# Second feed-forward product in three groups of 8, 8 and 6 hidden chunks, all by seven products, the last group ordered by token half

## The chip, the cores and the metric

The kernel runs on one core of a Trainium2 chip. The metric is the time of one execution on the device in microseconds. The three runs shown took 1502.62, 1504.49 and 1505.2 us; their median is 1504.49 us. All traces and rows below are from one profiled execution.

## The reference

One block of a streaming encoder, batch 1, 1024 tokens, width 1024, float32. A gated mixing sub-layer comes first, then the feed-forward sub-layer, whose end the change touches, and a last normalisation:

```python
h2 = rms_norm(x, norm_ffn_g[l]) * (1.0 + sc2) + sh2
a, bgate = jnp.split(jnp.einsum('bsd,df->bsf', h2, w_ffn_in[l]), 2, axis=-1)
x = x + g2 * jnp.einsum('bsf,fd->bsd', jax.nn.silu(a) * bgate, w_ffn_out[l])
...
return rms_norm(x, final_norm_g)
```

The hidden width is 2816, that is 22 chunks of 128. The second einsum (2816 to 1024) is "the second feed-forward product".

## The kernel before

Activations lie transposed: 128 channels on the partitions, tokens along the free axis, in two token halves of 512. Every float32 operand is split into a rounded high part and a low rest, and one product of 128x128 weights with 128x512 activations is three matmuls: weight high with activation high (L283), weight high with activation low (L284), weight low with activation high (L286). ScalarE makes the high part of a weight tile `wh` (L205), VectorE the low part `wl` (L206), from a loaded tile `raw`. The pools `wh` and `wl` have three buffers each, and `next_w` prepares weights two products ahead (`AHEAD = 2`).

Large products are made by **seven products** in the place of eight (Strassen's scheme, in the variant that shares its sums). A 2x2 block product has output rows (two blocks of output channels) and columns (two token halves); the seven are named by the characters of `PRODUCTS = "1265734"`. `product` (L295) makes one of them for two output chunks p = 0 and 1, over a number of hidden chunk pairs, in a PSUM bank: 1, 6, 7 and 4 accumulate in a bank called x, 2 in y, 5 and 3 in z. After each, VectorE adds the bank's content, scaled, to the residual tile `x1[j]` (L1013, called an evacuation here). Products 1 and 2 complete output chunk j = 2d + p in the first token half and 4 completes chunk j + 4 there; 6 and 3 go to chunk j, 5 and 7 to chunk j + 4, in the second half (d, 0 or 1, is the pair of output chunks). The next product that accumulates in a bank must wait for the evacuation before it.

The feed-forward part runs in these steps. (1) The first feed-forward product: eleven pairs of hidden chunks, N_IN = 11, seven products each, 24 matmuls a product (`in_product`). After a pair, `hid_set` (L932) forms the seven activation operands of the second product from its results, splits each into a staging tile (pool `stage`, three buffers; ScalarE L322, VectorE L323) and stores it to DRAM by a DMA that GpSimd (POOL) issues (L930). (2) The residual x1 is loaded again from DRAM: chunks 0 and 1 early, chunks 4, 5, 2, 3, 6 and 7 by six DMAs of POOL (L1006), after `hid_set` of the last pair. (3) The second product for hidden chunks 0 to 17, in three groups of three pairs: `group_load` (L961) brings a group's operands, two tiles `th` and `tl` for each pair and product, from DRAM by POOL's queue (L956), and then come seven products of 18 matmuls for d = 0 and seven for d = 1. The tiles `th`, `tl` come from a pool `t` of 58 buffers, which the operands of step 1 (56 tiles) and all the groups share; group 0's loads follow the first feed-forward product's last pair, product by product. (4) The last four hidden chunks (18 to 21) are multiplied directly (L1055, `piece_out`), in three pieces of the tokens, `PIECES = [(0, 512), (512, 256), (768, 256)]`: 12 matmuls for each of eight output chunks j and each piece.

With a piece's eighth chunk the last normalisation of that piece begins: ScalarE has squared the outputs (L1067), VectorE summed the squares (L1076), a matmul with ones sums over partitions (`ss`, L1104), ScalarE takes the reciprocal root and VectorE refines it in two steps (`rft` L1113, `rf` L1115). Then `piece_scale` (L1078) multiplies each chunk by `rf`: in pieces 0 and 1 all eight chunks on POOL (L1092), in the last piece chunks 0, 3 and 5 on POOL and five on VectorE (L1094). The results leave by DMAs of SyncE (L1097). Piece i is normalised while piece i + 1 is being multiplied.

The order on each engine is laid down when the kernel is built: a scheduler places instructions by priority and readiness, and each engine then takes its own list strictly in order. POOL's DMAs share eight semaphores in turn, so a DMA waits in the list until the eighth before it has landed.

## Time and profile before

| what | us |
|---|---|
| median of the runs (1502.62 to 1505.2) | 1504.49 |
| the profiled execution, its own time | 1502.96 |
| its span in the trace | 1501.2 |
| what lies around the span | 1.76 |
| busy: PE, VectorE, ScalarE, POOL | 1469.3, 1141.0, 623.1, 538.2 |

Times in rows are microseconds from the span's start. PE is TensorE, DVE VectorE, ACT ScalarE, POOL GpSimd and SP SyncE. A timeline row gives start, duration, engine, line, operation, output<-input and shape; in brackets stands how long the engine was idle before it and what ended that. Matmuls are pipelined, so that a row of 0.39 us and the next one's start overlap: the pitch, from start to start, is what a matmul costs.

### The profile page before, as it was taken

How to read it: one execution, taken by the hardware profiler on the slowest of the kernel's cores; microseconds unless marked ns; L12 is line 12 of the kernel's file. 1: busy time of each engine (PE TensorE's matmuls, PEld its weight loads, DVE VectorE, ACT ScalarE, POOL GpSimd, SP SyncE). 2: the span in 40 equal slices, each digit the busy share in tenths (PEclk: the TensorE clock that was granted, in tenths of full speed). 3: DMA queues.
4: the chain of work that ended last, by engine and by line, in shares of the span. 5: the costliest groups of instructions: out<-in, count | busy, mean ns of one | idle time of the engine just before them, and what ended most of it. 6: DMA issues, size and time to landing. Idle time of an engine off the chain costs nothing.

```text
span 1501.2 us, 17711 instructions
## 1 busy us (share of the span) xinstructions
PE 1469.3 (98%) x6455; PEld 1202.0 (80%) x6455; DVE 1141.0 (76%) x1569; ACT 623.1 (42%) x896; POOL 538.2 (36%) x467
## 2 busy tenths in 40 slices
PE   6999999999999999999999989999999999999997
PEld 2788888888888788887788868888888888888887
DVE  7994999887887984777767789776666665667755
ACT  4653433443343353244345454444444443222235
POOL 0037777777767773410121001111000016444005
PEclk9999999999999999999999989999999999999999
DMA  9522223232222268555765337544444449998403
GB/s 352 207 64 74 94 71 112 70 108 75 98 71 85 99 261 299 167 175 175 231 207 183 126 98 236 200 169 153 152 149 150 153 148 351 364 324 256 141 28 112
DMA packets 82697, 247.24 MB, mean 165 GB/s; under 512 B 9521, under 2 KB 11697, under 8 KB 82610
## 3 DMA queue, kind: packets, MB, share of 16 engines
q1 hardware_dynamic: 41776, 137.91, 27.4%
q0 software_dynamic: 36944, 95.44, 19.2%
q10 hardware_dynamic: 3890, 12.78, 2.2%
q8 instruction: 50, 0.82, 0.2%
q14 instruction: 37, 0.30, 0.1%
HBM read 183.69 MB, written 62.39 MB: 164 GB/s over the span
## 4 chain that ended last, share of the span: by engine, by line
PE 93%; DVE 4%; issue 1%; ACT 1%; DMA 1%; POOL 0%; POOLq 0%; ACTq 0%; DVEq 0%
PE x L286 11%; PE x L284 11%; PE x L283 10%; PE z L283 7%; PE z L284 7%; PE z L286 7%; PE y L284 6%; PE y L283 6%; PE y L286 6%; PE ya L284 2%; PE mix L286 2%; PE mix L284 2%; PE ya L283 2%; PE ya L286 2%; PE mix L283 2%; PE yb L283 2%
## 5 line engine op out<-in xcount | busy, mean ns | idle before, releaser
L205 ACT CAST wh<-raw 128x1024 fp32r<-128x1024 f32 (+2 forms) x257 | 259.4, 1010 | 482.8 <-PE z L284 122.0
L206 POOL TENSOR_TENSOR wl<-raw,wh 128x1024 fp32r<-128x1024 f32 x92 | 227.2, 2471 | 131.1 <-ACT wh L205 130.9
L206 DVE TENSOR_TENSOR wl<-raw,wh 128x1024 fp32r<-128x1024 f32 (+2 forms) x165 | 188.4, 1142 | 52.7 <-ACT wh L205 50.0
L671 DVE SCALAR_TENSOR_TENSOR c<-diff,vec,c 128x512 f32<-128x512 f32 x248 | 178.6, 751 | 3.3
L930 POOL DMA_DIRECT2D hid<-stage x71 | 37.9, 534 | 358.7 <-DVE stage L323 353.0
L283 PE MATMUL x<-th,wh 128*128 128x512 f32 x240 | 93.4, 389 | 0.0
L284 PE MATMUL x<-tl,wh 128*128 128x512 f32 x240 | 93.4, 389 | 0.0
L286 PE MATMUL x<-th,wl 128*128 128x512 f32 x240 | 93.4, 389 | 0.0
L671 DVE SCALAR_TENSOR_TENSOR c<-u,wsum,c 128x512 f32<-128x512 f32 x112 | 84.1, 751 | 1.8
L264 DVE CUSTOM_DVE_ANT_0 raw<-raw,cs,vec 128x1024 f32<-128x1024 f32 x24 | 35.5, 1486 | 50.6 <-DMA raw<-in_ada 50.6
L283 PE MATMUL z<-th,wh 128*128 128x512 f32 x168 | 65.4, 389 | 0.0
L284 PE MATMUL z<-tl,wh 128*128 128x512 f32 x168 | 65.4, 389 | 0.0
L286 PE MATMUL z<-th,wl 128*128 128x512 f32 x168 | 65.4, 389 | 0.0
L228 POOL TENSOR_TENSOR raw<-raw 128x1024 f32<-128x1024 f32 x12 | 29.8, 2482 | 95.0 <-DVE wl L206 94.2
L322 ACT CAST stage<-g 128x512 fp32r<-128x512 f32 x62 | 38.3, 621 | 52.0 <-DMA hid<-stage 25.1
L323 DVE TENSOR_TENSOR stage<-g,stage 128x512 fp32r<-128x512 f32 x62 | 42.5, 688 | 20.5 <-ACT stage L322 20.4
L956 POOL DMA_DIRECT2D th<-hid x71 | 38.1, 537 | 52.0 <-PE x L286 28.3
L283 PE MATMUL yb<-zsh,wh 128*128 128x512 f32 x128 | 50.0, 391 | 2.8 <-DVE gb L793 2.8
L283 PE MATMUL x<-t2h,wh 128*128 128x512 f32 x120 | 47.7, 400 | 5.1 <-ACT wh L205 2.8
L286 PEld LDWEIGHTS x<-th,wl 128*128 128x128 f32 x240 | 45.1, 188 | 9.4
L283 PEld LDWEIGHTS x<-th,wh 128*128 128x128 f32 x240 | 45.1, 188 | 9.3
L284 PEld LDWEIGHTS x<-tl,wh 128*128 128x128 f32 x240 | 45.1, 188 | 9.3
(1012 smaller groups left out, 4263.8 us busy)
## 6 DMA issues: line engine op xcount, KB each, us to landing
hid<-stage POOLq DMA_DIRECT2D x71, 512.0 KB, 4.0
raw<-in_w_fi SPq DMA_DIRECT2D x50, 512.0 KB, 4.3
raw<-in_w_duals SPq DMA_DIRECT2D x48, 512.0 KB, 3.5
th<-hid POOLq DMA_DIRECT2D x71, 256.0 KB, 5.9
tl<-hid POOLq DMA_DIRECT2D x71, 256.0 KB, 6.0
ada<-in_ada SPq DMA_DIRECT2D x24, 512.0 KB, 5.8
raw<-in_ada SPq DMA_DIRECT2D x24, 512.0 KB, 4.5
raw<-in_w_fo SPq DMA_DIRECT2D x24, 384.0 KB, 6.2
```

Of the source, the lines that this page charges most:

```text
L205: nc.scalar.copy(wh, raw)
L206: lo = lo_engine.tensor_tensor(wl, raw, f32(wh), ALU.subtract)
L228: eng.tensor_tensor(a["s1"], a["21"], a["22"], ALU.add)
L264: nc.vector.tensor_tensor_reduce(out=raw, in0=raw, in1=cs, scale=1.0, scalar=col(V_ADA, b), op0=ALU.mult, op1=ALU.add, accum_out=modc(b),)
L283: nc.tensor.matmul(ps, wh, xh, start=first, stop=False, skip_group_check=again)
L284: nc.tensor.matmul(ps, wh, xl, start=False, stop=False, skip_group_check=again)
L286: mm3.ins = nc.tensor.matmul(ps, wl, xh, start=False, stop=last, skip_group_check=again).ins
L322: nc.scalar.copy(hi, src)
L323: nc.vector.tensor_tensor(lo, src, f32(hi), ALU.subtract)
L671: tap.ins = nc.vector.scalar_tensor_tensor(out=out, in0=src[:, s : s + H], scalar=wt, in1=acc, op0=ALU.mult, op1=ALU.add).ins
L930: nc.gpsimd.dma_start(hid_dram[key], s)
L956: nc.gpsimd.dma_start(t, hid_dram[key][:, s])
```

## The change

The four direct chunks go. All 22 hidden chunks are now taken by seven products, in groups of four, four and three pairs: a product of groups 0 and 1 has 24 matmuls in the place of 18, its weight tiles are 128x1024 in the place of 128x768, and a group brings 56 operand tiles in the place of 42. `hid_set` makes seven stores for each of the eleven pairs (before, four for the last two). The last group has an order of its own: for d = 0 and then d = 1 the products 1, 2, 6, 7 and 4, which complete the first token half in all eight chunks, then product 5 for both d, then product 3, which is made in two pieces of 256 tokens (72 matmuls of 128x256). Its weights come by `last_units`, which loads some blocks again. Piece 0's sums are complete after product 4 and its scaling stands behind the second product 5; pieces 1 and 2 now hold four output chunks' products each.

```diff
-GROUP, GROUPS = 3, 3
-REST = 2 * GROUP * GROUPS
+GROUPS = [range(4), range(4, 8), range(8, 11)]
+LAST_ORDER = [(d, m) for d in range(2) for m in "12674"] + [(d, m) for m in "53" for d in range(2)]
...
+    def last_units(mats, n):
+
+        a = {}
+
+        def unit(m):
+            get = lambda i: load(mats[i], n)
+            add = lambda o, b: nc.vector.tensor_tensor(o, o, b, ALU.add)
+            if m == "6":
+                s, a21, t = get(3), get(2), get(0)
+                add(s, a21)
+                add(a21, t)
+                add(t, s)
+                a["7"] = a21
+            elif m == "5":
+                t, a21 = get(3), get(2)
+                add(t, a21)
+                a["5"] = t
+            elif m == "3":
+                t, a11 = get(1), get(0)
+                add(t, a11)
+                add(t, a["5"])
+            else:
+                t = a[m] if m in a else get("12_4".index(m))
+            return split_w(t, n)
+
+        return {m: (lambda m=m: unit(m)) for m in PRODUCTS}
...
     def hid_set(d):
 
         (b11, b12), (b21, b22) = ((ha[2 * d + p, "4"], ha[2 * d + p, "6"]) for p in range(2))
-        if 2 * d >= REST:
-            for p, half in enumerate(((b11, b12), (b21, b22))):
-                for h in range(2):
-                    store((2 * d + p, h), half[h])
-            return
...
     def group_load(g, m):
-        to[g, m] = [t_load((g * GROUP + i, m)) for i in range(GROUP)]
+        to[g, m] = [t_load((d, m)) for d in GROUPS[g]]
...
-    hid = {}
-    n = 2 * GROUP * P
...
-    for g in range(GROUPS):
-        for d in range(2):
-            banks = {}
-            for m in PRODUCTS:
-                product(banks, m, to[g, m], out_evac(d))
-                if d == 0 and m == "1":
-                    if g < GROUPS - 1:
-                        for q in PRODUCTS:
-                            group_load(g + 1, q)
-                    else:
-                        for h in range(2):
-                            for f in range(REST, FC):
-                                hid[f, h] = t_load((f, h))
-
-
-    ws = {}
-    for f in range(REST, FC, 2):
-        for oh in range(2):
-            raw = load(w_last[(f - REST) // 2, oh])
-            for d in range(2):
...
+    w_fo = [w_fo0, w_fo1, w_fo2]
+    fo_order = [[(d, m) for d in range(2) for m in PRODUCTS]] * 2 + [LAST_ORDER]
+    for g, order in enumerate(fo_order):
+        n = 2 * len(GROUPS[g]) * P
+        units = [(last_units if g == 2 else dual_units)([w_fo[g][d, m] for m in range(4)], n) for d in range(2)]
+        plan += [units[d][m] for d, m in order]
+
+    def out_product(g, d, m):
+        product(fo_banks[g, d], m, to[g, m], out_evac(d))
+
+    fo_banks = {(g, d): {} for g in range(3) for d in range(2)}
+    for g in range(2):
+        for d, m in fo_order[g]:
+            out_product(g, d, m)
+            if (d, m) == (0, "1"):
+                for q in PRODUCTS if g == 0 else "1267453":
+                    group_load(g + 1, q)
...
-    def piece_out(i, j):
-        at, n = PIECES[i]
-        h, off = at // H, at % H
-        o = ps_tile("y")[:, :n]
-        for f in range(REST, FC):
-            xs = tuple(t[:, off : off + n] for t in hid[f, h])
-            c0 = (j % 4) * P
-            mm3([o], slice(c0, c0 + P), ws[f, j // 4], [xs], f == REST, f == FC - 1)
...
-        evac = nc.vector.scalar_tensor_tensor(out=dst, in0=o, scalar=modc(40 + j), in1=dst, op0=ALU.mult, op1=ALU.add)
...
             load_rsqrt(act.ins)
...
+        for k in range(i, i + (n + PIECES[i][1] - 1) // PIECES[i][1]):
...
-    for i in range(len(PIECES)):
-        acc, sqs = sqs[0] if i else None, []
-        lag = LAG if i == LAST else 0
-        for j in range(KC):
-            piece_out(i, j)
-            if j > lag and j - lag < KC - APART * (i == LAST):
-                piece_sum(i, j - lag)
-            if i and j == NORM_AT:
-                norm = piece_norm(i - 1, [acc])
-            if i and j == NORM_AT + 2:
-                with tc.issue_after(piece_out.ins):
-                    rf = piece_rstd(i - 1, *norm)
-                piece_scale(i - 1, rf)
-    piece_scale(LAST, piece_rstd(LAST, *piece_norm(LAST, [sqs[0]] + sqs[KC - APART :])))
...
+    norm = rf = None
+    for d, m in LAST_ORDER[:-2]:
+        out_product(2, d, m)
+        for p in range(2):
+            j = 2 * d + p
+            if m == "2":
+                piece_square(0, j)
+                if j:
+                    piece_sum(sqs[0, 0], sqs[0, j])
+            elif m == "4":
+                piece_square(0, KH + j)
+                piece_sum(sqs[0, 0], sqs[0, KH + j])
+            elif m == "5":
+                piece_square(1, KH + j, H)
+                if j:
+                    piece_sum(sqs[1, KH], sqs[1, KH + j])
+        if (d, m) == (0, "5"):
+            norm = piece_norm(0, [sqs[0, 0]])
+        elif (d, m) == (1, "5"):
+            piece_scale(0, piece_rstd(0, *norm))
+    last = [next_w(), next_w()]
+    for i in (1, 2):
+        at, n = PIECES[i]
+        off = at - H
+        acc = sqs[1, KH][:, off : off + n]
+        for j in range(KH):
+            ps = fo_banks[2, j // 2]["z", j % 2][:, off : off + n]
+            for k, (hi, lo) in enumerate(to[2, "3"]):
+                c0 = (j % 2 * len(to[2, "3"]) + k) * P
+                xs = hi[:, off : off + n], lo[:, off : off + n]
+                mm3([ps], slice(c0, c0 + P), last[j // 2], [xs], False, k == len(to[2, "3"]) - 1, True)
+            dst = x1[j][:, at : at + n]
+            nc.vector.scalar_tensor_tensor(out=dst, in0=ps, scalar=modc(40 + j), in1=dst, op0=ALU.mult, op1=ALU.add)
+            piece_square(i, j)
+            if i < LAST or j < KH - APART:
+                piece_sum(acc, sqs[i, j])
+            if i == LAST and j == NORM_AT:
+                norm = piece_norm(1, [sqs[1, KH][:, : PIECES[1][1]]])
+            if i == LAST and j == NORM_AT + 1:
+                piece_scale(1, piece_rstd(1, *norm))
+    piece_scale(LAST, piece_rstd(LAST, *piece_norm(LAST, [acc] + [sqs[LAST, j] for j in range(KH - APART, KH)])))
```

In the rows below, taken from the lists of the built programs, the numbers behind names tell buffers apart.

**The six loads of x1 on POOL.** Here `hidN_m` is a stored operand of pair N for product m, `th`/`tl` are tiles of group 1, and `x14` to `x17` are x1's chunks 4 to 7 (`x12` chunk 2). Before:

```order
L956 DMA th_9878<-hid3_1_7749 128x512
L956 DMA tl_9879<-hid3_1_7749 128x512
L930 DMA hid21_1_9805<-stage_9802 128x1024
L956 DMA th_9882<-hid4_1_8038 128x512
L956 DMA tl_9883<-hid4_1_8038 128x512
L956 DMA th_9886<-hid5_1_8327 128x512
L1006 DMA x14_9822<-x1_dram4_5820 128x1024
L1006 DMA x15_9823<-x1_dram5_5821 128x1024
```

And of the change:

```order
L978 DMA th_9952<-hid4_1_8038 128x512
L957 DMA hid10_5_9856<-stage_9853 128x1024
L957 DMA hid10_7_9862<-stage_9859 128x1024
L957 DMA hid10_3_9867<-stage_9864 128x1024
L978 DMA tl_9953<-hid4_1_8038 128x512
L957 DMA hid10_4_9873<-stage_9870 128x1024
L978 DMA th_9956<-hid5_1_8327 128x512
L978 DMA tl_9957<-hid5_1_8327 128x512
L1028 DMA x14_9890<-x1_dram4_5820 128x1024
L1028 DMA x15_9891<-x1_dram5_5821 128x1024
```

Ahead of x1's chunk 4 there now stand all seven stores of the last pair, and the tiles `th_9956` and `tl_9957`. These two take the buffers of group 0's first operand tiles (`th_9534`, `tl_9535` below), so they wait until PE has used those for the last time, which is in product 1 of d = 1; `tl_9957` waits for that product's 15th matmul.

**The middle of group 0 on PE.** The banks are x (`x_9938` for d = 0, `x_10265` and `x_10279` for d = 1), y (`y_10297`, d = 1) and z (`z_10017` before, `z_10131` after, d = 0). Before, product 3 of d = 0 follows product 7:

```order
L286 MATMUL x_9867<-th_9701,wl_9989 128x512
L283 MATMUL z_10017<-th_9733,wh_10013 128x512
L284 MATMUL z_10017<-tl_9734,wh_10013 128x512
L286 MATMUL z_10017<-th_9733,wl_10014 128x512
L283 MATMUL z_10017<-th_9737,wh_10013 128x512
```

In the change product 1 of d = 1 and the first 13 matmuls of its product 2 stand between:

```order
L313 MATMUL x_9938<-th_9741,wl_10097 128x512
L310 MATMUL x_10265<-th_9534,wh_10197 128x512
L311 MATMUL x_10265<-tl_9535,wh_10197 128x512
L310 MATMUL x_10279<-th_9534,wh_10197 128x512
L311 MATMUL x_10279<-tl_9535,wh_10197 128x512
L313 MATMUL x_10265<-th_9534,wl_10198 128x512
...
L310 MATMUL y_10297<-th_9594,wh_10227 128x512
L311 MATMUL y_10297<-tl_9595,wh_10227 128x512
L310 MATMUL z_10131<-th_9773,wh_10127 128x512
```

Products 3 and 4 of d = 0 have moved behind these 37 matmuls, while their weights already hold two of the three buffers of `wh` and of `wl`.

**Piece 0's normalisation on VectorE.** `sq` are squares, `ss`, `rq`, `rft` and `rf` the steps of the root. Before, the steps stand among piece 1's evacuations (L1064) of chunks 3 and 4, with 12 evacuations of 256 tokens still to come:

```order
L1064 SCALAR_TENSOR_TENSOR x13_9821<-y_11396,mod_103,x13_9821 128x256
L1076 TENSOR_TENSOR sq_11351<-sq_11351,sq_11392 128x256
L1113 SCALAR_TENSOR_TENSOR rft_11414<-ss_11372,rq_11374 128x512
L1076 TENSOR_TENSOR sq_11351<-sq_11351,sq_11410 128x256
L1115 SCALAR_TENSOR_TENSOR rf_11373<-rft_11414,rf_11373 128x512
L1064 SCALAR_TENSOR_TENSOR x14_9822<-y_11433,mod_103,x14_9822 128x256
```

In the change they stand behind the last evacuation of product 5 of d = 1 (`z_11406`), ahead of the first of product 3's eight:

```order
L1035 SCALAR_TENSOR_TENSOR x17_9893<-z_11406,ng2_9875,x17_9893 128x512
L1083 TENSOR_TENSOR sq_11371<-sq_11371,sq_11417 128x512
L1120 SCALAR_TENSOR_TENSOR rft_11425<-ss_11379,rq_11381 128x512
L1083 TENSOR_TENSOR sq_11371<-sq_11371,sq_11421 128x512
L1122 SCALAR_TENSOR_TENSOR rf_11380<-rft_11425,rf_11380 128x512
L1157 SCALAR_TENSOR_TENSOR x10_9879<-z_11349,mod_103,x10_9879 128x256
```

What follows `rf` has become shorter: eight evacuations of 256 tokens in the place of twelve. POOL's list behind it is the same as before: eight passes of 128x512, eight of 128x256 and three of 128x256 for the last piece.

More of the change, by code (lines that the diff above doesn't have):

```diff
@@ L108, in block_kernel @@
 def block_kernel(ctx: ExitStack, tc: tile.TileContext, x0, xT, c, vecs, ada, w_first, w_plain, w_duals,
-                 w_short, w_conf, w_o, w_fi, w_fo, w_last, outT):
+                 w_short, w_conf, w_o, w_fi, w_fo0, w_fo1, w_fo2, outT):
     nc = tc.nc
@@ L1188 @@
         "w_fi": _duals(w_fi, [[FC + f for f in range(FC)], list(range(FC))], [range(KC // 2), range(KC // 2, KC)]),
-        "w_fo": np.stack([_duals(w_fo, [range(4), range(4, 8)], [range(f, f + 2 * GROUP, 2), range(f + 1, f + 2 * GROUP, 2)])
-                          for f in range(0, REST, 2 * GROUP)]),
-        "w_last": w_fo[REST * P :].reshape(-1, 2, P, 2, H).transpose(0, 3, 2, 1, 4).reshape(-1, 2, P, 1024),
+        **{f"w_fo{g}": _duals(w_fo, [range(4), range(4, 8)], [[2 * d + h for d in ds] for h in range(2)])
+           for g, ds in enumerate(GROUPS)},
     }
```

26 lines of the change are left out of this document (11 added, 15 removed).

## Prediction, written before the change was run

> **What bounds the kernel now.** I read the page's first line and its chain first, then windows and timelines of the two places that the change touches.
>
> ```profile
> span 1501.2 us, 17711 instructions
> PE 1469.3 (98%) x6455; PEld 1202.0 (80%) x6455; DVE 1141.0 (76%) x1569; ACT 623.1 (42%) x896; POOL 538.2 (36%) x467
> PE 93%; DVE 4%; issue 1%; ACT 1%; DMA 1%; POOL 0%; POOLq 0%; ACTq 0%; DVEq 0%
> ```
>
> PE is the bound: busy 98% of the span and 93% of the chain that ends last. So matmuls taken away count in full, unless something else is late in their place. The two places:
>
> ```profile
> 1235.00:1273.45 38.45, 38.45 (x171) 31.84 (x170) 20.58 (x26) 14.97 (x23) 22.66 (x43) 1.00 1.07 331
> 1273.45:1293.85 20.40, 20.40 (x91) 16.90 (x90) 11.68 (x16) 6.24 (x10) 10.24 (x20) 1.00 1.12 385
> 1471.00:1491.00 20.00, 20.00 (x166) 19.84 (x165) 14.36 (x28) 12.77 (x28) 13.80 (x12) 1.00 0.30 114
> 1491.00:1501.20 10.20, 1.93 (x10) 1.29 (x8) 3.40 (x8) 1.77 (x5) 5.20 (x8) 0.80 0.54 190
> ```
>
> Columns: window, length, busy time of PE, PEld, DVE, ACT and POOL, granted clock, DMA share, GB/s. Until 1491 PE is never idle. Around group 0's start (1273.45) all 16 DMA engines are full, at 331 and 385 GB/s. The last 10.2 us have almost no PE work. The chain's own end:
>
> ```profile
> 1469.60 0.87 PE ss L1104 x2
> 1481.98 0.60 PE ss L1104 x2
> 1488.69 5.41 POOL y L1092 x7
> 1494.11 1.17 issue
> 1495.27 0.77 POOLq L1199
> 1496.04 1.37 POOL y L1092 x2
> ```
>
> POOL's scaling is already the last part of the chain: it has next to nothing to spare, although it is busy 36% of the whole.
>
> **Part A: fewer matmuls.**
>
> ```profile
> 1273.45 0.39 PE L283 MATMUL x<-th,wh 128*128 128x512 f32 x1
> 1277.53 0.39 PE L283 MATMUL y<-th,wh 128*128 128x512 f32 x1
> 1482.66 0.28 PE L286 MATMUL y<-th,lwl 128*128 128x256 f32 x1
> 1490.92 0.28 PE L286 MATMUL y<-th,lwl 128*128 128x256 f32 x1
> ```
>
> From the first row to the second lie 18 matmuls: pitch 0.2267 us. From the third to the fourth lie 69: pitch 0.1197 us. Before, from 1273.45 on: 42 products of 18 are 756, and the direct chunks add 96 of 512 and 192 of 256 tokens: 171.4 + 21.8 + 23.0 = 216.1 us. After: 28 products of 24 and 12 of 18 are 888, and product 3 is 72 of 256: 201.3 + 8.6 = 209.9 us. **Part A is −6.2 us.**
>
> **Part B: POOL's passes become the tail's bound.**
>
> ```profile
> 1475.94 10.79 POOL L1092 TENSOR_TENSOR x<-x,rf 128x512 f32<-128x512 f32 x8 [82.49 <-DVE rf L1115]
> 1487.99 6.11 POOL L1092 TENSOR_TENSOR y<-x,rf 128x256 f32<-128x256 f32 x8 [1.26 <-DVE rf L1115]
> 1495.31 2.10 POOL L1092 TENSOR_TENSOR y<-x,rp 128x256 f32<-128x256 f32 x3 [1.20 <-ACT rp L1083]
> 1474.18 0.69 DVE L1113 SCALAR_TENSOR_TENSOR rft<-ss,rq 128x512 f32<-128x512 f32 x1
> 1475.11 0.68 DVE L1115 SCALAR_TENSOR_TENSOR rf<-rft,rf 128x512 f32<-128x512 f32 x1
> ```
>
> POOL's list behind piece 0's `rf` is unchanged: 10.79 + 6.11 + 2.10 = 19.0 us of passes. Before, it begins at 1475.94, 15.1 us ahead of PE's last direct matmul (1490.92 + 0.12 = 1491.04), and its gaps of 1.26 and 1.20 us are its slack. The change puts the start behind the second product 5, with only product 3 (8.6 us of PE) to cover it. Without a stall that product ends at 1273.45 + 201.3 + 0.9 (two `ss` matmuls, as in the chain) = 1475.6. Then `rf` needs the last evacuation (0.75, L1013's length below), a sum of squares (0.69), `rft` (0.69), another sum (0.69) and `rf` (0.68), in VectorE's order as shown above, with 0.2 of hand-over: **3.7 us**. Then 0.15, 19.0 of passes without a gap, and 3.8 from the end of POOL's last pass to the span's end, as before (1495.31 + 2.10 = 1497.41 to 1501.2). End: 1475.6 + 26.65 = 1502.3. Bounded by PE it would be 1475.6 + 8.6 + 0.6 (the second `ss` pair) + 10.2 = 1495.0. So POOL gives back 7.3 us, and **A and B together are +1.1 us**. Unknown are the 3.7 us: 3.4 if every step follows without a gap, 4.6 if ScalarE's root adds 0.9 that the sums don't hide.
>
> [...]
>
> **Part S: a stall in the middle of group 0.** These six loads of x1 fed product 5 of d = 0:
>
> ```profile
> 1274.98 1.07 POOL L930 DMA_DIRECT2D hid<-stage  x2 [0.72 <-DVE stage L323]
> 1284.33 0.56 POOL L1006 DMA_DIRECT2D x<-x_dram  x1
> 1288.28 2.62 POOL L1006 DMA_DIRECT2D x<-x_dram  x5 [3.39 <-issue]
> DMA to landing us min/median/max: 6.0/7.7/8.8
> 1292.50 0.75 DVE L1013 SCALAR_TENSOR_TENSOR x<-z,ng,x 128x512 f32<-128x512 f32 x1 [4.95 <-DMA x<-x_dram]
> 1293.85 0.39 PE L283 MATMUL z<-th,wh 128*128 128x512 f32 x1
> ```
>
> Chunk 4 was issued at 1284.33 and evacuated bank z (p = 0) at 1292.50 to 1293.25, after 4.95 us of VectorE waiting for it. PE wanted the bank at 1293.85: a margin of 0.60 us, with no wait on PE. In the change these loads stand behind seven stores and behind `tl_9957`, which waits for the 15th matmul of product 1 of d = 1. Product 3 of d = 0, which needs bank z, comes only 22 matmuls later.
>
> ```profile
> L206 DVE TENSOR_TENSOR wl<-raw,wh 128x1024 fp32r<-128x1024 f32 x15 | 18.4, 1223 | 13.8 <-ACT wh L205 13.4
> L205 ACT CAST wh<-raw 128x1024 fp32r<-128x1024 f32 x15 | 15.8, 1051 | 23.8 <-PE z L284 13.4 <-PE x L284 5.6 <-PE y L284 4.5
> ```
>
> Step by step: products 1, 2, 6, 5 and 7 of d = 0 are 120 matmuls and end at 1273.45 + 27.2 = 1300.65. Two of three buffers of `wh` and `wl` hold the postponed weights of 3 and 4, so the weights of product 1, d = 1, can be made only then: 1.05 us of cast, then 1.22 of low part, of which PE's first matmuls cover 0.9: 1.05 + 0.3 or so. VectorE makes that low part behind the staging of the last store, which I put at 0.8 us more. Product 2 of d = 1 meets the same want of a buffer: some 1 us again. The place and the count come from the order, the prices from the rows: about **3 us** of PE idle. `tl_9957` is then free at about 1307 (1300.65 + 2.2 + 15 × 0.2267, and its issue), x1's chunk 4 is issued at about 1307.4, and lands 6.0 to 8.8 us later by the row above; that was beside full queues, and 512 KB took 3.5 to 4.0 elsewhere:
>
> ```profile
> hid<-stage POOLq DMA_DIRECT2D x71, 512.0 KB, 4.0
> raw<-in_w_duals SPq DMA_DIRECT2D x48, 512.0 KB, 3.5
> hid<-stage POOLq DMA_DIRECT2D x8, 512.0 KB, 5.5
> ```
>
> With 4 to 8 us and 0.75 of evacuation the bank is free at 1312.2 to 1316.2. PE reaches product 3 at 1300.65 + 3 + 37 × 0.2267 = 1312.0. That adds 0 to 4 us. I take 2, nearest to the 5.5 of stores in this stage, so **S = 5 us** (3 to 7). What could lengthen it: the first of the seven stores. Until it can be issued, 54 tiles of 256 KB, 6 stores and 7 weight tiles of 512 KB, 21 MB, must pass from 1238.2 on. At 385 GB/s that takes 54.5 us. Then the seven are spread as VectorE stages them; in an earlier pair they went out like this:
>
> ```profile
> 1198.22 0.53 POOL L930 DMA_DIRECT2D hid<-stage  x1 [23.25 <-DVE stage L323]
> 1202.49 1.74 POOL L930 DMA_DIRECT2D hid<-stage  x3 [3.74 <-DVE stage L323]
> 1207.24 0.53 POOL L930 DMA_DIRECT2D hid<-stage  x1 [3.02 <-DVE stage L323]
> 1211.36 0.53 POOL L930 DMA_DIRECT2D hid<-stage  x1 [2.23 <-DVE stage L323]
> ```
>
> 13.1 us from first to last issue. If the first goes out at 1285 to 1288, the last does by 1301 and `tl_9957` decides. If it comes later, the loads come later one for one.
>
> [...]
>
> **What costs nothing.** Six more stores (0.53 us of POOL each) lie in the first product, where POOL waits 23 us for staging. Weight tiles of 1024 cost cast 1051 ns against 5.4 us of PE a product. The last group's VectorE work has little room:
>
> ```profile
> L206 DVE TENSOR_TENSOR wl<-raw,wh 128x768 fp32r<-128x768 f32 x42 | 39.9, 951 | 0.8 <-ACT wh L205 0.8
> ```
>
> 14 low parts and 12 weight sums of this width by 0.95, 24 evacuations by 0.75 and 10 sums of squares by 0.69 are 49.6 us, some 45 from start to start (a row overlaps the next by about 0.08), beside 12 × 18 × 0.2267 = 49 us of PE. It fits if each evacuation comes within the 2 us that the other chunk's nine matmuls give it. If that cover is too thin, products there start 0 to 2 us late; I add nothing, since the range has room for it.
>
> **Sum.** Span 1501.2 + 1.1 + 5 = 1507.3; own time 1502.96 + 6.1 = 1509.1. The median of the runs shown is 1.5 above the profiled one, so 1510.6; rounded down, for VectorE's gaps, to **1510.0**.
>
> **Rivals**, in own time of a profiled execution.
>
> R1, not slower: POOL keeps up. If the 19 passes took up to 11.7 us in the place of 19.0, PE would set the tail, 1495.0 in the span without a stall; with a stall of 3 to 5 us that is 1499.8 to 1501.8. Against it stands POOL's row, 1.35 us a pass of 512; the price of 7.3 us falls away from 0.83 us a pass on. For it: only that POOL has 1.2 us idle twice. Chance 0.08, half of it faster than before by over 0.2%, that being about what a measurement of this kernel can tell from no change.
>
> R2, the stall is small: x1 lands in 4 us and VectorE makes the low parts at once, S = 0 to 2, 1504 to 1506. Against it: two buffers are held. 0.10.
>
> R3, the loads come later: stores first at 1291 to 1296, by 363 GB/s or VectorE's staging beside the evacuations; S = 8 to 14, 1512 to 1518. For it: 4.95 us of waiting already, and the mean of the windows above, 350 GB/s. 0.22.
>
> R4, the change does only what the count says: no stall, POOL not late, 1496.8. POOL's rows and the order speak against it. 0.05.
>
> Forecast, S = 3 to 7, 1507 to 1511: 0.55.
>
> **How the numbers follow.** 0.2% of 1504.5 is 3.0 us: 1501.5 and 1507.5 in medians, 1500.0 and 1506.0 in own time. Faster: R4 and about half of R1, 0.08. Same: the rest of R1, R2, 0.15. Slower: the forecast and R3, 0.77. The range 1503.5 to 1517 leaves out R4, R1 and the top third of R3, 0.20 in all.
>
> **What would show it.** A: 888 matmuls of 512 at 0.2267 from group 0's start, 72 of 256 behind them. B: POOL's 19 passes without a gap of over 0.3 us at the end, on the chain of waits. S: PE idle some 1 us ahead of products 1 and 2 of d = 1 in group 0, released by ScalarE's `wh`, and 1 to 4 us ahead of product 3, released by VectorE's evacuation that waits for x1. It is wrong if POOL idles in the tail, if PE shows no such gaps, or if new gaps lie in groups 1 or 2.

## The result, and the profile after

The changed kernel takes 1516.52 us in the median of four runs (1513.58 to 1518.51), against 1504.76 before: the ratio is 1.0081, with a 95% interval of 1.0068 to 1.0094. The forecast was 1510.0. The profiled execution took 1516.64 us, its span is 1514.9; the forecast for it was 1509.1.

The page's first lines and the shares of the chain of waits, of the changed kernel:

```profile
span 1514.9 us, 17567 instructions
PE 1468.0 (97%) x6371; PEld 1195.8 (79%) x6371; DVE 1147.0 (76%) x1556; ACT 625.1 (41%) x890; POOL 547.1 (36%) x485
PE 92%; DVE 4%; issue 1%; ACT 1%; DMA 1%; POOL 1%; SPq 0%; POOLq 0%; DVEq 0%; ACTq 0%
```

PE has 84 instructions less and is busy 1.3 us less, not 6.2, in a span that is 13.7 us longer. The place of the loss is in the waits of PE from 1260 to 1330 (columns: waiting group, what ended the wait, total, count, longest) and in four windows of the second product (columns as before). Before, PE had no waits there at all.

```profile
PE x L310 <- ACT wh L205: 6.3, 1, 6.3
PE y L310 <- ACT wh L205: 0.9, 1, 0.9
```

```profile
1274.59:1301.79 27.20, 27.20 (x121) 22.34 (x119) 15.23 (x20) 6.72 (x9) 14.36 (x28) 1.00 1.19 397
1301.79:1308.26 6.47, 0.16 (x1) 0.00 (x1) 5.93 (x8) 3.90 (x6) 2.14 (x4) 0.90 0.72 255
1308.26:1314.36 6.10, 6.10 (x16) 4.85 (x16) 2.43 (x3) 0.00 (x0) 1.07 (x2) 0.55 0.81 238
1489.36:1514.90 25.54, 11.26 (x82) 10.14 (x81) 14.97 (x27) 9.77 (x24) 18.38 (x19) 0.80 0.45 165
```

Five products of d = 0 run without a gap. Then PE is idle for 6.5 us, and behind that the granted clock is 0.55: 15 matmuls take 6.1 us where 3.4 would do. The fourth window, from the end of the last product 5 to the span's end, is POOL's: 18.4 us of 19 passes.

What PE waited for stands on ScalarE and POOL. First ScalarE's timeline of the changed kernel, then POOL's (start, duration, engine, line, operation; in brackets the idle time before and what ended it):

```profile
1281.06 1.05 ACT L205 CAST wh<-raw 128x1024 fp32r<-128x1024 f32 x1
...
1290.94 1.05 ACT L205 CAST wh<-raw 128x1024 fp32r<-128x1024 f32 x1 [4.39 <-PE x L311]
1301.42 0.62 ACT L349 CAST stage<-g 128x512 fp32r<-128x512 f32 x1 [9.43 <-DMA hid<-stage]
1301.95 1.04 ACT L205 CAST wh<-raw 128x1024 fp32r<-128x1024 f32 x1
1302.89 0.61 ACT L349 CAST stage<-g 128x512 fp32r<-128x512 f32 x1
1303.91 0.62 ACT L349 CAST stage<-g 128x512 fp32r<-128x512 f32 x1 [0.41 <-DMA hid<-stage]
1306.64 0.62 ACT L349 CAST stage<-g 128x512 fp32r<-128x512 f32 x1 [2.11 <-DVE stage L350]
1307.17 1.04 ACT L205 CAST wh<-raw 128x1024 fp32r<-128x1024 f32 x1
```

```profile
1294.88 1.70 POOL L957 DMA_DIRECT2D hid<-stage  x3 [1.29 <-DMA th<-hid]
...
1303.66 0.53 POOL L957 DMA_DIRECT2D hid<-stage  x1 [6.40 <-DVE stage L350]
...
1315.35 3.16 POOL L1028 DMA_DIRECT2D x<-x_dram  x6
```

The first three stores of the last pair were staged by 1282.3, but POOL issues them at 1294.88, behind group 0's loads. There are three staging buffers, so the fourth staging cast (1301.42) waits for the first store to land. The weights' casts stand behind the staging casts on ScalarE. The one for product 1 of d = 1 is the last shown: three more staging casts (1302.89, 1303.91 and 1306.64) stand between, so it comes at 1307.17, and PE goes on at 1308.26. The buffer that it writes, product 7's, was free at 1301.7, when PE had read it for the last time.

The tail, on POOL:

```profile
1492.70 10.87 POOL L1099 TENSOR_TENSOR x<-x,rf 128x512 f32<-128x512 f32 x8 [57.62 <-DVE rf L1122]
1503.53 5.51 POOL L1099 TENSOR_TENSOR y<-x,rf 128x256 f32<-128x256 f32 x8
1508.99 2.09 POOL L1099 TENSOR_TENSOR y<-x,rp 128x256 f32<-128x256 f32 x3
```

The gaps of 1.26 and 1.20 us of before are gone, and POOL works from `rf` to the end without a break.

### The profile page after: what moved, and what is told of

It reads as the page before. It is cut to its first block, busy times and chain, and to the rows that moved or that the text cites. A ratio compares the mean times of both kernels' runs of the same rounds, so it can differ in the third digit from the quotient of the medians.

```text
span 1514.9 us, 17567 instructions
## 1 busy us (share of the span) xinstructions
PE 1468.0 (97%) x6371; PEld 1195.8 (79%) x6371; DVE 1147.0 (76%) x1556; ACT 625.1 (41%) x890; POOL 547.1 (36%) x485
## 4 chain that ended last, share of the span: by engine, by line
PE 92%; DVE 4%; issue 1%; ACT 1%; DMA 1%; POOL 1%; SPq 0%; POOLq 0%; DVEq 0%; ACTq 0%
PE x L313 11%; PE x L311 11%; PE x L310 11%; PE z L310 7%; PE z L311 7%; PE z L313 7%; PE y L313 5%; PE y L311 5%; PE y L310 5%; PE mix L310 2%; PE mix L313 2%; PE ya L313 2%; PE ya L310 2%; PE ya L311 2%; PE mix L311 2%; PE yb L310 1%
## 5 line engine op out<-in xcount | busy, mean ns | idle before, releaser
L206 DVE TENSOR_TENSOR wl<-raw,wh 128x1024 fp32r<-128x1024 f32 (+2 forms) x165 | 196.0, 1188 | 57.7 <-ACT wh L205 54.0
L310 PE MATMUL x<-th,wh 128*128 128x512 f32 x272 | 107.4, 395 | 7.4 <-ACT wh L205 7.3
L311 PE MATMUL x<-tl,wh 128*128 128x512 f32 x272 | 106.9, 393 | 0.0
L313 PE MATMUL x<-th,wl 128*128 128x512 f32 x272 | 106.4, 392 | 0.0
L310 PE MATMUL z<-th,wh 128*128 128x512 f32 (+1 forms) x196 | 74.3, 379 | 0.0
L313 PE MATMUL z<-th,wl 128*128 128x512 f32 (+1 forms) x196 | 73.7, 376 | 0.0
L311 PE MATMUL z<-tl,wh 128*128 128x512 f32 (+1 forms) x196 | 73.7, 376 | 0.0
L311 PEld LDWEIGHTS x<-tl,wh 128*128 128x128 f32 x272 | 51.8, 190 | 10.7
L310 PE MATMUL y<-th,wh 128*128 128x512 f32 x140 | 54.6, 390 | 0.9 <-ACT wh L205 0.9
L311 PE MATMUL y<-tl,wh 128*128 128x512 f32 x140 | 54.5, 389 | 0.0
```

The lines of the kernel that those rows point to most:

```text
L206: lo = lo_engine.tensor_tensor(wl, raw, f32(wh), ALU.subtract)
L310: nc.tensor.matmul(ps, wh, xh, start=first, stop=False, skip_group_check=again)
L311: nc.tensor.matmul(ps, wh, xl, start=False, stop=False, skip_group_check=again)
L313: mm3.ins = nc.tensor.matmul(ps, wl, xh, start=False, stop=last, skip_group_check=again).ins
```

## The experiments

Executions of one kernel differ from their median by up to 3.5 us either way, and group 0's first matmul starts anywhere from 1271.8 to 1277.1 although PE's work ahead of it is the same. So beside the median there is, for each profiled execution, the **stretch** from group 0's first matmul to the span's end. For the kernel before it is 1501.2 - 1273.45 = 227.75 us, for the changed one 1514.9 - 1274.59 = 240.3. The stretch is one execution's too: the stall in group 0 is 6.3, 6.4 and 7.9 us in three kernels that are alike there (changed, tail_split, tail_psum), so differences of 1 to 2 us say little by themselves. Each ratio is to executions of the kernel before that were taken beside that run (medians 1503.33 to 1504.76), so medians of different rows compare only roughly. And the scheduler lays down all lists anew for every kernel: an edit can move more than the lines that it shows.

| kernel | median us | ratio to before, 95% interval | stretch us |
|---|---|---|---|
| changed | 1516.52 | 1.0081, 1.0068 to 1.0094 | 240.3 |
| stores_act | 1518.81 | 1.0103, 1.0087 to 1.0119 | 244.0 |
| stores_first | 1513.01 | 1.0062, 1.0046 to 1.0079 | 235.4 |
| groups_344 | 1515.40 | 1.0080, 1.0060 to 1.0101 | 239.0 |
| before_441 (one execution) | 1517.50 | - | 238.6 |
| tail_split | 1515.40 | 1.0085, 1.0066 to 1.0103 | 237.05 |
| tail_psum | 1512.41 | 1.0051, 1.0035 to 1.0067 | 236.3 |
| first_split_443 | 1508.62 | 1.0031, 1.0019 to 1.0042 | 232.9 |
| first_split_344 | 1513.85 | 1.0060, 1.0040 to 1.0080 | 238.7 |
| adds_behind | 1509.63 | 1.0041, 1.0028 to 1.0054 | 233.65 |
| x1_earlier | 1509.09 | 1.0033, 1.0018 to 1.0048 | 232.8 |
| busy_wait | 1508.36 | 1.0036, 1.0023 to 1.0049 | 230.9 |
| busy_wait_tail | 1507.77 | 1.0024, 1.0014 to 1.0033 | 231.3 |

By medians alone most single edits are not told apart from the changed kernel; their verdicts rest on the stretch and on the waits in the trace.

### The stores by another queue

```diff
-        nc.gpsimd.dma_start(hid_dram[key], s)
+        if key[0] == N_IN - 1:
+            nc.scalar.dma_start(f32(hid_dram[key]), f32(s))
+        else:
+            nc.gpsimd.dma_start(hid_dram[key], s)
```

> The changed kernel, but the last hidden pair's seven stores are issued by ScalarE's queue in the place of POOL's, so that they no longer stand behind group 0's loads. Nothing else is edited; the bytes are the same. Theory Q (order in POOL's list): the stores, issued at 1294.88 in the changed kernel, go out from about 1278 on, ScalarE's fourth staging cast no longer waits 9.4 us for one to land, PE's stall of 6.3 us ahead of product 1 of d = 1 in group 0 falls to 1 to 2 us and the 14 matmuls at 0.427 us behind it go; 1516.5 becomes about 1508 (1506 to 1510). Theory V (volume: 21 MB through full DMA queues, whatever the order): the loads take the stores' time, the stall only moves, 1514 to 1517. Theory X (the prediction's last wait, for x1's chunk 4): the stall turns into one ahead of product 3 of d = 0, 1511 to 1514.

It became no faster (stretch 244.0, and the intervals of the ratios overlap), a miss for theory Q as put. Waits of PE, then ScalarE's fifth staging cast and POOL's first load of x1:

```profile
PE z L310 <- issue: 5.0, 1, 5.0
PE z L310 <- ACT wh L205: 3.7, 1, 3.7
```

```profile
1292.53 0.62 ACT L349 CAST stage<-g 128x512 fp32r<-128x512 f32 x1 [7.53 <-DMA hid<-stage]
```

```profile
1306.39 0.53 POOL L1031 DMA_DIRECT2D x<-x_dram  x1 [2.72 <-DVE wl L206]
```

The stores did leave early (1278.5 and 1284.5), but of the three that left together at 1284.45, while loads were under way, none freed a buffer before 1292.5, 8 us later (the kernel before has medians of 4.0 us over all its stores and 5.5 in this stage), and ScalarE waited 7.53 us for it, ahead of the weights that product 5 needed. Chunk 4 of x1, issued 9 us earlier than in the changed kernel (1315.35), was still too late: in this build product 3 of d = 0 stands directly behind product 7, PE was there at 1309.5, and the 5.0 us are its wait for that chunk's evacuation. Freeing one list moved the wait; a part of theory V holds, though the time lies above its 1514 to 1517.

### The stores ahead of the last loads

```diff
-        if d == N_IN - 1:
+        if d == N_IN - 1 and m not in "34":
             group_load(0, m)
...
             hid_set(d)
+    for m in "34":
+        group_load(0, m)
```

> The changed kernel, but group 0's operand loads for products 3 and 4 are written behind the last pair's stores in the place of ahead of them. POOL issues all, the bytes are the same. Theory Q: the stores go out at about 1283, the stall ahead of product 1 of d = 1 falls from 6.3 to 1 to 2 us, 1507 to 1510; products 3 and 4 might wait 0 to 2 us for their operands. Theory V: no gain, 1514 to 1518, with the wait now on the operands of product 3. Theory X: x1's loads come no earlier, a stall of 3 us or more ahead of product 3, 1511 to 1514.

Waits of PE from 1260 to 1330:

```profile
PE x L313 <- DVE wl L206: 2.1, 1, 2.1
PE x L310 <- ACT wh L205: 0.9, 1, 0.9
PE z L310 <- DVE x L1037: 0.8, 1, 0.8
```

The 6.3 us became 0.9, and 4.9 us went from the stretch, by order alone, with the same bytes and on one queue. In the build product 2 of d = 1 also no longer has matmuls ahead of product 3. What is left is what the prediction had listed, a weight cast that waits for a buffer (0.9), a low part (2.1), and x1 (0.8, a wait for the evacuation). But the low part waits for something else than it said: VectorE has a weight sum ahead of it, for which it waited 3.89 us for a weight tile to land. The median, 1513.01, misses theory Q's 1507 to 1510. The matmuls behind the low part were slow here, too. VectorE ends the low part at 1305.34 and the evacuation, for which PE waited 0.8 us, at 1311.91:

```profile
1304.12 1.22 DVE L206 TENSOR_TENSOR wl<-raw,wh 128x1024 fp32r<-128x1024 f32 x1
...
1311.16 0.75 DVE L1037 SCALAR_TENSOR_TENSOR x<-z,ng,x 128x512 f32<-128x512 f32 x1 [4.57 <-DMA x<-x_dram]
```

Less that wait an estimated 5.7 us are left for 17 matmuls (their number is that in first_split_443, which has this edit too); at 0.2267 they need 3.9. Some 8 of them at 0.427, an estimated 3.5 us, make the difference.

### Loads or stores: two sizes

```diff
-GROUPS = [range(4), range(4, 8), range(8, 11)]
+GROUPS = [range(3), range(3, 7), range(7, 11)]
```

> The changed kernel with its groups of 3, 4 and 4 pairs in the place of 4, 4 and 3: group 0 loads 42 tiles as the kernel before did, but the last pair still makes seven stores, and product 3 at the end has 96 matmuls of 256 tokens. Theory Q: the stores are still behind the loads but come about 8 us earlier, while group 0's product 7 ends 6.8 us earlier, so the stall of 6.3 us stays at 4 to 6; the longer product 3 covers 2.9 us more of POOL's passes: 1511 to 1514. Theory V: 12 loads (3.1 MB, 8 us) less ahead of group 0 take the stall away, and with the 2.9 us of the tail 1503 to 1507.

For the other, the kernel before got groups of 4, 4 and 1 pairs (its operands and weights cut to match):

```diff
-GROUP, GROUPS = 3, 3
-REST = 2 * GROUP * GROUPS
+GROUPS = [range(4), range(4, 8), range(8, 9)]
+REST = 18
```

> The kernel before with its three groups of 4, 4 and 1 pairs in the place of 3, 3 and 3: the same chunks by seven products, the same direct chunks and four stores a pair at the end, but group 0 loads 56 tiles and its products have 24 matmuls. PE keeps product 3 of d = 0 ahead of d = 1. The third group has products of 6 matmuls, for which the weights cannot be made in time, so only group 0 is compared. Theory Q+L (what blocks group 0 is that the last pair's stores and x1's loads stand behind the group's loads): with only four stores they still go out near 1290 to 1295, x1's chunk 4 is loaded some 8 us later than in the kernel before, and PE waits 4 to 9 us ahead of product 3 of d = 0 (or for the weights that ScalarE casts behind the fourth staging), at 1295 to 1302. Theory N (the number of stores, seven with three staging buffers, makes the stall): with four stores there is less than 1.5 us of waiting in group 0.

Waits of PE in group 0 (1260 to 1330), of groups_344 and of before_441:

```profile
PE x L313 <- DVE wl L206: 2.2, 1, 2.2
PE x L310 <- DVE x L1035: 1.8, 1, 1.8
PE x L310 <- ACT wh L205: 1.3, 1, 1.3
PE y L310 <- ACT wh L205: 0.7, 1, 0.7
PE z L310 <- DVE x L1035: 0.7, 1, 0.7
```

```profile
PE z L283 <- issue: 4.1, 1, 4.1
```

With 42 loads and seven stores PE waits 6.7 us; with 56 loads and four stores 4.1; with both 7.2; with neither, before, not at all. Either kernel waits, though they differ from the kernel before in more than the count: groups_344 has the changed kernel's order on PE, before_441 longer products. By the number theory Q+L (4 to 9 us) holds and N does not; groups_344, at 1515.40, lies outside the ranges of both its theories. The same staging wait is in both traces, 6.98 us on ScalarE in groups_344 and this in before_441:

```profile
1296.54 0.62 ACT L322 CAST stage<-g 128x512 fp32r<-128x512 f32 x1 [7.48 <-DMA hid<-stage]
```

Two things in these traces go against a single cause. In groups_344 the first three stores go out at 1278.82, 16 us earlier than in the changed kernel, and the fourth staging cast still waits until 1287.82: there it is the 9 us that the stores take to land, beside the loads, and not their place in POOL's list. And in before_441 the staging wait does not reach PE. The evacuation of x1's chunk 4 stands on VectorE behind a weight sum whose weight tile was late:

```profile
1306.60 1.22 DVE L228 TENSOR_TENSOR raw<-raw 128x1024 f32<-128x1024 f32 x1 [5.46 <-DMA raw<-in_w_fo]
1307.74 0.74 DVE L1013 SCALAR_TENSOR_TENSOR x<-z,ng,x 128x512 f32<-128x512 f32 x1
```

Stores, weight tiles and x1 are late in one kernel or another; which of them PE meets first depends on the order.

Groups of 3, 4 and 4 add a wait of 3.9 us near the start of the last group, ahead of product 7 of d = 0; VectorE's list had waited 5.72 us for a weight tile there. So they don't pay.

### POOL's tail

```diff
-        return i < LAST or j in POOL_LAST
+        return not i or j in (POOL_LAST if i == LAST else (0, 2, 4, 6))
...
-        if i == LAST:
+        if i:
             rp = wide_tile("rp")[:, :n]
...
-        out = ps2_tile("rf")[:, :n] if i == LAST else r
+        out = ps2_tile("rf")[:, :n] if i else r
```

> The changed kernel, but four of piece 1's eight scaling passes are made by VectorE in the 1.9 us that it idles between the two last roots; group 0 is untouched. Theory P (POOL's passes set the tail): POOL ends four passes of 0.69 us earlier, 2.8 us off the span, 1513 to 1514.5. Theory D (the tail is set by the squares, sums and roots of the last piece, POOL only ends beside them): less than 0.5 us, 1516 to 1517.

The stretch is 3.25 us shorter; the stall in group 0 is as in the changed kernel (6.4). From POOL's start (behind `rf`) to the end it is 20.2 us in the place of 22.2: 2.0 of the 2.8 us that theory P expected, and four times what theory D allows. The other 1.2 us lie ahead of `rf`. The medians (1515.40, between the ranges of the two theories, and 1516.52) do not tell the two kernels apart. Then the squares:

```diff
+        summed = i and n is None and (i < LAST or j < KH - APART)
...
-        sqs[i, j] = sq = wide_tile("sq")[:, :n]
+        sqs[i, j] = sq = (ps2_tile if summed else wide_tile)("sq")[:, :n]
```

> The kernel of tail_split, with the squares that VectorE sums in the last two pieces written to PSUM in the place of SBUF, so that these sums have one input in SBUF. Theory K (a VectorE operation with both inputs in SBUF waits for POOL's pass): the sums of 128x256 beside POOL's passes, 1.1 to 1.3 us each in tail_split, fall to 0.4 to 0.5, PE's wait of 1.7 us ahead of the ss matmul goes, and piece 1's root comes 2 to 3 us earlier; the end gains little, 0.3 to 1 us, because POOL's passes already had only 0.35 us of idle time. Theory M (the sums are long for another reason, such as ScalarE's late squares): their duration stays at 1 us or more.

The sums on VectorE from 1488 to 1506, in tail_split and in tail_psum (busy time, mean ns of one):

```profile
L1083 DVE TENSOR_TENSOR sq<-sq 128x256 f32<-128x256 f32 x5 | 5.2, 1054 | 0.1
```

```profile
L1084 DVE TENSOR_TENSOR sq<-sq 128x256 f32<-128x256 f32 x5 | 2.1, 412 | 0.1
```

One input in PSUM in the place of SBUF, and a sum beside POOL's passes takes 412 ns, not 1054: theory K's figure, not M's. In the kernel before, sums with both inputs in SBUF took 0.41 to 0.43 us while POOL was idle (the three from 1470.61 to 1474.78, ahead of POOL's start at 1475.94). That the long sums wait for POOL's pass is theory K's reading; the rows show the lengths. POOL gains too, as it would if it had waited for VectorE as well: its eight passes of 128x512 take 10.31 us, not 11.25 as in tail_split.

```profile
1491.38 10.31 POOL L1100 TENSOR_TENSOR x<-x,rf 128x512 f32<-128x512 f32 x8 [55.19 <-DVE rf L1123]
1501.63 4.83 POOL L1100 TENSOR_TENSOR y<-x,rp 128x256 f32<-128x256 f32 x7
```

From `rf` to the end it is 1510.3 - 1491.38 = 18.9 us, against 20.2 in tail_split (1490.72 to 1510.9) and 22.2 in the changed kernel. This run's stall in group 0 happened to be 7.9 us.

### The edits together

The diffs of stores_first, tail_split and tail_psum in one kernel:

> The changed kernel with three edits together: stores ahead of the loads of products 3 and 4 (stores_first), four of piece 1's passes on VectorE (tail_split) and the squares in PSUM (tail_psum). If the stall in group 0 and POOL's tail are two separate causes, their gains add: 3.5 (stores_first) and about 3 (tail_split, by its trace) off 1516.5, 1509 to 1511. If the tail waits for something that the stall hides, less than 4 off in all, 1513 or more.

The gains add, roughly: 7.4 us of the stretch are gone, where stores_first took 4.9 and tail_psum 4.0 alone. The median is 7.9 below the changed kernel's, and the intervals of the two ratios are apart. The stall in group 0 and POOL's tail are two separate causes. In this run 4.5 us of waiting for a low part are left in group 0: VectorE has a weight sum ahead of it, whose weight tile came late.

The same, and the diff of groups_344:

> The same three edits with groups of 3, 4 and 4 pairs. Group 0 has 12 loads less and the stores come first, so little of its 9 us of waits and slow matmuls in groups_344 should stay (1 to 4 us); the wait of 3.9 us for weights at the start of the last group, and its slow matmuls, stay. 1504 to 1508; if the stores' place is not what makes the waits in group 0, 1512 or more.

A miss: 1513.85 lies where the expectation put it if the stores' place is not what makes the waits. The low part's wait is 5.8 us here, behind the same kind of late weight tile (VectorE waited 7.25 us for it), and the last group's wait 4.3. Less loading did not help, perhaps because the smaller group's products are shorter too; no run tests that.

### What is late next

On top of first_split_443, for the two weight units of group 0 (`split_w.ins` is the last low part written ahead of it):

```diff
-    def dual_units(mats, n, early=False, eng=nc.vector):
+    def dual_units(mats, n, early=False, eng=nc.vector, ordered=False):
...
             if m == "6":
+              with ExitStack() as behind:
+                if ordered:
+                    behind.enter_context(tc.issue_after(split_w.ins))
```

> first_split_443 with one order more: the weight sums of product 6, d = 1, in group 0 stand on VectorE behind the low part of product 1's weights and not ahead of it (there VectorE waited for late weight tiles, and PE 4.5 us for that low part). Theory X (behind it, x1's chunk 4 is late too, as the prediction had it): the 4.5 us wait goes, and PE waits 3 to 5 us ahead of product 3 of d = 0 for the evacuation instead; 1507 to 1510, no clear gain. Theory W (the late weight tiles were the only thing left): all waits in group 0 fall below 2 us and the slow matmuls go, 1502 to 1504.

The waits of PE, and the evacuation that PE waited for:

```profile
PE z L314 <- DVE x L1041: 5.3, 1, 5.3
PE x L314 <- ACT wh L205: 1.0, 1, 1.0
```

```profile
1312.44 0.75 DVE L1041 SCALAR_TENSOR_TENSOR x<-z,ng,x 128x512 f32<-128x512 f32 x1 [8.67 <-DMA x<-x_dram]
```

Theory X: the 4.5 us of the low part are gone, and 5.3 us for x1's chunk 4 ahead of product 3 have come in their place. The stretch is the same within 0.8 us.

On top of adds_behind:

```diff
-    for m in "34":
-        group_load(0, m)
+    group_load(0, "3")
...
     for j in (4, 5, 2, 3, 6, 7):
         nc.gpsimd.dma_start(x1[j], x1_dram[j])
+        if j == 5:
+            group_load(0, "4")
```

> adds_behind with x1's chunks 4 and 5 loaded ahead of group 0's operands of product 4. The built order then keeps products 3 and 4 of d = 0 ahead of d = 1, so nothing is postponed and no weight buffers are held. Theory X (the time at which x1's chunk 4 lands decides): it is issued at about 1300 in the place of 1306, and PE waits 3 to 6 us ahead of product 3, at 1300.7; 1505 to 1509. Theory V2 (the bytes that must pass before product 3, some 24 MB from 1238 on at 385 GB/s, are through only at about 1300, whatever the order): the same wait, and moving it further brings nothing. If x1 alone had been in the way, less than 2 us of waits are left, 1501 to 1504.

```profile
1295.32 0.54 POOL L1033 DMA_DIRECT2D x<-x_dram  x1 [1.48 <-DMA hid<-stage]
...
1303.98 0.75 DVE L1042 SCALAR_TENSOR_TENSOR x<-z,ng,x 128x512 f32<-128x512 f32 x1 [8.06 <-DMA x<-x_dram]
```

Counted from group 0's first matmul, x1's chunk 4 is issued 9.7 us earlier than in adds_behind and evacuated 6.1 us earlier. It lands 8.7 us behind its issue, and PE still waits 5.6 us, since product 3 is now next in line. This fits V2, an argument and not a proof. In this kernel 46 operand tiles and 13 stores stand ahead of chunk 4 on POOL; with 7 weight tiles on the other queue and the chunk itself they are 23 MB. The traffic from 1238 until chunk 4's evacuation (last column, GB/s):

```profile
1238.00:1304.00 66.00, 61.24 (x271) 50.39 (x269) 39.55 (x51) 24.10 (x33) 35.00 (x66) 0.99 1.12 365
```

At 365 GB/s 23 MB take 63 us, until 1301. PE wants product 3 at 1299; nothing is left over for an order that is not perfect.

### The slow matmuls

22 matmuls on an operand already there fill that wait; they compute nothing that is used.

```diff
+        if (g, d, m) == (0, 0, "3"):
+            hi = to[0, "1"][0][0]
+            o = ps2_tile("y")
+            for _ in range(22):
+                nc.tensor.matmul(o, hi[:, :P], hi, start=True, stop=True)
```

> x1_earlier with 22 matmuls of 128x512 put on PE ahead of product 3 of d = 0 in group 0, where PE waited 5.6 us; they multiply an operand that is there already, and nothing reads what they write. Theory C (after some us of idling PE runs at half pace for a while: 9 or 10 matmuls at 0.427 us in the place of 0.227 in x1_earlier): the 22 take 5.0 us of the wait, less than 1 us of it is left, product 3 begins at the same time and runs at 0.227 from the start; 1.9 us less from group 0's first matmul to the end, 1507 median. Theory O (the slow pitch comes from the operands or the DMA traffic of that moment): the pitch stays 0.427 behind the fill, no gain, 1509.

Four us of product 3 from its first matmul, in x1_earlier and in busy_wait:

```profile
1304.84:1308.81 3.97, 3.97 (x9) 3.10 (x10) 3.20 (x4) 0.00 (x0) 2.82 (x6) 0.50 1.25 404
```

```profile
1308.93:1312.93 4.00, 4.00 (x18) 3.33 (x19) 3.86 (x5) 0.00 (x0) 2.83 (x6) 1.00 1.25 401
```

Nine matmuls at a granted clock of 0.50 against 18 at 1.00, at the same DMA rate: theory C, not O. Of the wait 0.9 us are left. The stretch is 1.9 us shorter, as expected, but that is within what one execution can show; the pace is the evidence.

Then, on top of it, two of piece 0's passes on VectorE (its root is copied for them as well):

```diff
-        return not i or j in (POOL_LAST if i == LAST else (0, 2, 4, 6))
+        return j in ((0, 1, 2, 4, 5, 6), (0, 2, 4, 6), POOL_LAST)[i]
...
```

> busy_wait with two of piece 0's eight passes of 128x512 on VectorE too. POOL's list in the tail is then 6 passes of 1.29 and 7 of 0.69, 12.6 us in the place of 15.1. Theory P: the end comes up to 1.5 us earlier, until PE's own end (10.2 us behind its last matmul of product 3, as in the kernel before) sets it; 1505 to 1507. Theory D: VectorE's two passes stand ahead of evacuations and squares' sums of product 3, PE or the roots wait for them, and the end does not move or comes later.

```profile
1489.08 7.84 POOL L1114 TENSOR_TENSOR x<-x,rf 128x512 f32<-128x512 f32 x6 [58.18 <-DVE rf L1137]
1498.20 2.77 POOL L1114 TENSOR_TENSOR y<-x,rp 128x256 f32<-128x256 f32 x4 [1.28 <-ACT rp L1104]
1501.57 2.09 POOL L1114 TENSOR_TENSOR y<-x,rp 128x256 f32<-128x256 f32 x3 [0.59 <-ACT rp L1104]
```

No gain, theory D: POOL idles again, 1.28 and 0.59 us, for roots that come later. POOL is no longer the bound there. No version tried is faster than the kernel before; the last is still at 1.0024 (1.0014 to 1.0033).

## Why the prediction was right in sign and short in size

**Part A held.** From group 0's first matmul to the end of the last product 5 there are 214.8 us: 201.3 of matmuls as counted, 0.9 of `ss`, and 12.6 of idling and slow matmuls, which belong to Part S.

**Part B held.** POOL began 3.3 us behind that product (3.7 and 0.15 forecast), its 19 passes took 18.4 us without a gap (19.0), and the end came 3.8 behind them: 25.5 us in the place of 26.65. Piece 1's passes took 0.69 us each, 5.51 in the place of the 6.11 us that the sum of 19.0 holds: they began at 1503.53, when VectorE's last sum was over (1499.97), where before (from 1487.99) they ran beside sums until 1490.78. What was missed is VectorE's side: its sums of 128x256 beside product 3 rose to 1.09 us in the mean (0.70 before), and PE waited 1.7 us for the last one; POOL being the bound, it cost nothing yet.

**Part S failed: 12.6 us in the place of 5, and in part by another path.** The first step that failed is "If the first goes out at 1285 to 1288, the last does by 1301 and `tl_9957` decides". Nothing in the prediction supports 1285 to 1288: its own bytes and rate, 54.5 us from 1238.2 on, put the first store at 1292.7, which is R3's case (1291 to 1296) and not the forecast's. It went out at 1294.88, and the rate until then was 363 GB/s, not 385:

```profile
1238.20:1294.88 56.68, 56.68 (x252) 46.94 (x251) 38.25 (x48) 20.85 (x29) 31.86 (x61) 1.00 1.14 363
```

The second is what a late store does: "the loads come later one for one", and PE was to meet that ahead of product 3. In the trace it met it at product 1 of d = 1. Through the three staging buffers the late store stops ScalarE, whose list holds the weights' casts. PE lost 6.5 us there, where this weight step was put at some 2.2; the one ahead of product 2 cost 0.9, as put. In stores_first, with the stores early, the wait for the cast is 0.9 us and that for the low part 2.1. x1's loads did come 8 us later (1315.35 in the place of 1307.4), but the wait for them, put at 0 to 4 us, did not show in the changed kernel, because PE reached product 3 only at 1320.9; it showed as soon as the other waits were taken away (5.3 us in adds_behind).

Two more terms were not in the sum. The slow matmuls behind the wait: 6.1 us for 15 that need 3.4, so 2.7 us. And 1.2 us in front of a product of the last group, where the prediction had named 0 to 2 and added nothing; a new gap there was one of its own signs of being wrong. The remaining 1.3 of the 12.6 us lie in small pieces. R3 (S of 8 to 14, chance 0.22) came about, for its reason in part, and 1516.64 lies in its 1512 to 1518; of R1, R2 and R4 none came.

That the range held, by 0.5 us, is luck. The 1517 at its end supposed medians 1.5 us above the profiled execution, so it stood for 1515.5 in own time, which the 1516.64 exceeds (and it left out 2.5 of R3's 6 us, not a third); in the changed kernel the median lies 0.1 below. The forecast also took group 0's start at 1273.45, as before; in the changed kernel's profile it is 1274.59, another 1.1 us, which is there already at the first store of the pair before the last (1236.30 and 1237.43).

The loss of 12.55 us in the stretch is thus, to 0.1 us, -6.2 of matmuls, +12.6 of Part S and +6.2 by POOL's tail (7.3 less the 1.1 us that the tail was shorter than forecast).

## What to carry to other kernels

When a change puts more loads ahead of a store on one queue, follow the store's buffer back to the engine that fills it, and then list everything that stands behind the filling there: here one late store stopped the casts of the weights. A wait on PE of several us can cost more than its length: here 9 matmuls behind a wait of 5.6 us (x1_earlier) and 12 behind one of 6.3 us (changed kernel) ran at 0.427 us in the place of 0.227; count both. Here transfers filled the DMA engines up to the moment of need (DMA share 1.19 at 397 GB/s in the changed kernel, 1.12 at 365 GB/s in x1_earlier), and reordering them helped only so far: it took 4.9 us off the stretch once (stores_first), and from then on moved the wait from one consumer to the next.

## What the runs showed of the hardware

PE's pace after a wait was 0.427 us a matmul of 128x512 in the place of 0.227. It lasted 5.3 us (12 matmuls, granted clock 0.50) behind a wait of 6.3 us in the changed kernel, 4.0 us (9, clock 0.50) behind one of 5.6 in x1_earlier, 3.5 us (8) behind one of 4.1 in before_441, and an estimated 3.5 us in stores_first, whose waits there are 0.9 and 2.1 us. Behind the wait of 2.4 us at 1450.81 in before_441 the pitch was 0.23 to 0.33 us at first and 0.427 from 1452.10 to 1455.09. Behind the single wait of 0.9 us at 1317.50 in the changed kernel the granted clock was 1.00 (until 1320.93).

```profile
1450.81 0.50 PE L283 MATMUL x<-th,wh 128*128 128x512 f32 x1 [2.40 <-ACT wh L205]
...
1452.10 0.63 PE L286 MATMUL x<-th,wl 128*128 128x512 f32 x1
1452.53 0.63 PE L283 MATMUL z<-th,wh 128*128 128x512 f32 x1
...
1455.09 0.56 PE L283 MATMUL x<-th,wh 128*128 128x512 f32 x1
```

A VectorE sum with both inputs in SBUF took 1054 ns beside POOL's passes and 412 ns with one input in PSUM, while POOL's eight passes of 128x512 went from 11.25 us (tail_split) to 10.31.
